# One wide matmul per weight block: a two-layer hybrid encoder whose column tiles stream both parts of the operand at once

## The chip, the cores and the metric

The kernel runs on one core of a Trainium2 chip. The metric is the device time of one execution in microseconds (us), of which the median over three runs is quoted. TensorE (PE) does the matmuls, VectorE (DVE) and ScalarE (ACT) the elementwise work, GpSimd (POOL) and SyncE (SP) mostly start transfers.

## The reference

Two identical layers and a final norm, on 256 tokens of 2048 channels. A layer normalises x, multiplies it by one wide input projection, feeds four token mixers (a short convolution A, attention B, a recurrence C in two directions, a convolution module D), projects each mixer's output, merges the four by sigmoid gates, and adds the output projection to x:

```python
h = rms_norm(x, norm_g)
proj = h @ w_in                      # 2048 x 15104, all mixers and gates
...
bp = jnp.einsum('bskc,kcd->bskd', ys, w_branch)
g = jax.nn.sigmoid(gates.reshape(b, s, N_BRANCH, D_MODEL) + b_gate)
merged = jnp.sum(g * bp, axis=2)
return x + merged @ w_out
```

All of it is float32 with a float32 accuracy.

## The kernel before

Everything is held channel-major: a tile is 128 channels by 256 tokens (`S` is 256). Weights come as a stream of chunks, each 128 x 1024 (512 KB): eight 128 x 128 blocks. A chunk is loaded into `raw`, ACT rounds it to `hi` (a float32r copy), and DVE makes `lo = raw - hi`; three `hi` and two `lo` buffers exist. The operand x is split in the same way into two float32r parts that lie side by side in a `slab`: `[128 channels, 4 tiles, hi | lo, 256 tokens]`.

A column tile (`tile_b`) is 128 output channels: two chunks, 16 blocks. For each block `passes` issues hi·x_hi and hi·x_lo, and after the eight blocks of a chunk lo·x_hi for each: 24 matmuls of 256 columns per chunk, all added up in one 256-column half of a PSUM bank. PSUM has eight banks: two under the tag `mg`, two under `mb`, four (`sd`) for the side computations. `tile_pair` puts two column tiles into the halves of one bank (gates and output projection), `tile_branch` does the same with one chunk for a mixer's projection (`mb`). Consumers read the PSUM tile directly.

The order of a layer's stream: three L tiles (low-rank inputs), the c_k, c_r, c_v tiles, k, v, the tiles of B and A, d_gate and d_val, then the merges M(0) and M(1) in turn, d_z, M(3) (mixer D's), c_z, M(2) (the recurrence's), and eight O pairs (output projection). The first tiles of a layer (`raw`) are computed from x before the norm and scaled by its reciprocal `rbc` afterwards.

Mixers are generators ("side computations"): after each main matmul `pump` lets one go on when a planner's clocks say that its inputs should be there, and when VectorE and ScalarE have little work ahead (`lead`). `drain` makes a merge wait in the planner until its mixer is finished. The planner's clock counts a matmul as columns / 2400 + 0.003 us. A scheduler then fixes the order on each engine; every engine runs its list strictly in order. `lo`/`hi` conversions carry high priority. All operations are recorded through one helper, so almost every row of the profile names its line, L199; the tile names tell the groups apart: `mg<-slab,hi` is a column tile's matmul with the weights' high part, `sd<-...` a side computation's, `arena<-mg` a read of a column tile out of PSUM.

Of the kernel before, what the change touches and what calls it, by code (L numbers as in the profile page):

```python
# [13 lines left out]
ALU = mybir.AluOpType  # L14
# [16 lines left out]
# columns of the per-channel parameter table  # L31
# [9 lines left out]
# columns of the constant table  # L41
# [14 lines left out]
def tile_order():  # L56
    """Column tiles of w_in that give channel-major outputs, in stream order."""
# [32 lines left out]
def stream_order():  # L90
    """The whole weight stream of a layer, in the order in which it is used."""
# [11 lines left out]
class Arena:  # L103
    """Addresses inside one SBUF tile, handed out and taken back in program order."""
# [12 lines left out]
    def get(self, words, keep=False, take=True):  # L117
        """keep: long-lived, from the bottom; others from the free run that fits best, if not just given back."""
# [4 lines left out]
        while i < self.n:  # L123
# [6 lines left out]
            if e - i >= m:  # L130
                # long-lived from the bottom, others from the top of the run that fits best
# [33 lines left out]
class Engine:  # L165
    """An engine of nc that keeps the clocks by which side computations are interleaved."""
# [43 lines left out]
class Kern:  # L210
# [39 lines left out]
    def a(self, shape, keep=False):  # L250
        words = int(np.prod(shape[1:]))
        if self.cur is None:
            # the main stream waits for side computations to give memory back
            t = self.now
            while not self.arena.get(words, keep, False) and self.now < t + 50:
                self.now += 0.2
                self.pump()
# [11 lines left out]
    def room(self, words):  # L269
        """Waits until the side computation that asks can have so much until it asks again."""  # L270
# [13 lines left out]
    def slab(self, shape, dt=F32):  # L284
        """8 KB per partition: operand tiles, and what the recurrence keeps until then."""
# [19 lines left out]
    # TensorE runs in program order. A side computation is a generator that yields before a step whose first  # L305
    # instructions use what the last step made; it goes on when that should be there: `now` is TensorE's clock,
    # `clk` when each engine has done what it was given, `due` when the step's results are there.
    def add(self, gen, lead=None):
        """lead: how much work VectorE and ScalarE may have before them when it goes on."""
        e = Side(gen, self.now, lead or self.LEAD)  # L310
        if self.cur:
            # a part of the computation that adds it, and so is its memory
# [5 lines left out]
    def rush(self):  # L318
        """What the recurrence waits for goes before other side computations."""
# [1122 lines left out]
```

## Time and profile before

| what | value |
|---|---|
| median of 3 runs | 2015.02 us (2013.86 to 2015.18) |
| profiled execution: span from its first to its last instruction | 2012.3 us |
| PE / PE weight loads | 1989.7 us (99%) / 1947.2 us (97%), 17122 of each |
| DVE | 1334.6 us (66%), 2143 instructions |
| ACT | 1176.3 us (58%), 2013 instructions |
| granted TensorE clock | 0.998, in all slices 9 of 10 or more: the 2.4 GHz level |
| traffic from HBM | 332.48 MB, 169 GB/s over the span |

How to read it: matmuls are pipelined, so the record of one is longer than the distance to the next. What a matmul costs in a stream is the distance between starts, which the timeline gives: a merged row has the start of its first record and the number of records, and the next row's start ends it.

### The profile page before, as it was taken

To read this page: it belongs to the slowest core of one execution; us is meant where nothing else is said; L and a number is where in the kernel's file an instruction comes from. 1 tells how busy PE (TensorE), PEld (TensorE's weight loads), DVE (VectorE), ACT (ScalarE), POOL (GpSimd) and SP (SyncE) were. 2 spreads that over 40 slices of the span, in tenths; PEclk is the share of its full clock that TensorE was granted. 3 is DMA by queue.
4 is the path that set the end of the run, shared out by engine and by line. 5 is a ranking of instruction groups with operands and counts; after the bars stand their busy time and mean duration, and the time that the engine had idled before them with its cause. 6 is when DMAs were issued, how large, how long until landed. Compare 5 with 4: busy or idle time off the path is not lost.

```text
span 2012.3 us, 41703 instructions
## 1 busy us (share of the span) xinstructions
PE 1989.7 (99%) x17122; PEld 1947.2 (97%) x17122; DVE 1334.6 (66%) x2143; ACT 1176.3 (58%) x2013; POOL 70.8 (4%) x115
## 2 busy tenths in 40 slices
PE   8999999999999999999999999999999999999997
PEld 7999999999999999999999999999999999999997
DVE  7666869866685445555676768797667845455554
ACT  6676665666546655444556766565764566544444
POOL 1001010000101000000000011000001100000000
PEclk9999999999999999999999999999999999999999
DMA  7555443445555445556655555444555634455553
GB/s 247 180 175 170 158 160 133 147 160 179 179 180 154 142 142 195 191 196 203 206 189 175 171 166 167 140 145 139 174 173 188 189 127 145 154 197 195 195 183 126
DMA packets 97727, 343.78 MB, mean 171 GB/s; under 512 B 11808, under 2 KB 12192, under 8 KB 97536
## 3 DMA queue, kind: packets, MB, share of 16 engines
q1 hardware_dynamic: 93312, 331.48, 49.3%
q0 software_dynamic: 3648, 8.59, 1.8%
q8 instruction: 134, 2.20, 0.4%
q10 hardware_dynamic: 576, 1.05, 0.1%
q14 instruction: 57, 0.47, 0.1%
HBM read 332.48 MB, written 8.39 MB: 169 GB/s over the span
## 4 chain that ended last, share of the span: by engine, by line
PE 98%; DVE 0%; ACT 0%; DMA 0%; issue 0%; DVEq 0%; SPq 0%; ACTq 0%
PE mg L199 78%; PE sd L199 10%; PE mb L199 10%; DMA arena<-xT 0%; DVE arena L199 0%; ACT slab L199 0%; DVE slab L199 0%; DVEq L1437 0%; ACT arena L199 0%; DVE lo L199 0%; ACT L178 0%; ACT hi L199 0%; SPq L199 0%; DVEq L199 0%; ACTq L199 0%
## 5 line engine op out<-in xcount | busy, mean ns | idle before, releaser
L199 PE MATMUL mg<-slab,hi 128*128 128x256 f32 x8704 | 1182.4, 285 | 9.7 <-ACT slab L199 8.6
L199 PEld LDWEIGHTS mg<-slab,hi 128*128 128x128 f32 x8704 | 1098.8, 192 | 20.9 <-ACT slab L199 8.6
L199 DVE TENSOR_TENSOR lo<-raw,hi 128x1024 fp32r<-128x1024 f32 x612 | 748.8, 1224 | 550.4 <-PE mg L199 372.3
L199 ACT ACTIVATE hi<-raw 128x1024 fp32r<-128x1024 f32 x612 | 646.9, 1058 | 647.5 <-PE mg L199 495.7
L199 PE MATMUL mg<-slab,lo 128*128 128x256 f32 x4352 | 636.0, 285 | 0.0
L199 PEld LDWEIGHTS mg<-slab,lo 128*128 128x128 f32 x4352 | 568.8, 192 | 5.6 <-issue 3.4
L199 DVE TENSOR_TENSOR arena<-arena 128x512 f32<-128x512 f32 (+18 forms) x365 | 156.1, 433 | 17.2 <-ACT arena L199 6.6
L199 DVE SCALAR_TENSOR_TENSOR arena<-arena,par 128x256 f32<-128x256 f32 x346 | 152.6, 478 | 6.4 <-ACT arena L199 4.9
L199 PE MATMUL mb<-slab,hi 128*128 128x256 f32 x1088 | 154.8, 284 | 0.0
L199 PEld LDWEIGHTS mb<-slab,hi 128*128 128x128 f32 x1088 | 141.0, 191 | 0.4
L199 PE MATMUL mb<-slab,lo 128*128 128x256 f32 x544 | 90.8, 286 | 0.0
L178 ACT ACT_TABLE_LOAD x62 | 79.5, 1283 | 16.6 <-PE sd L199 15.1
L199 ACT ACTIVATE arena<-arena 128x256 f32<-128x256 f32 (+4 forms) x155 | 77.5, 521 | 12.9 <-DVE arena L199 10.9
L199 PEld LDWEIGHTS mb<-slab,lo 128*128 128x128 f32 x544 | 75.8, 192 | 0.8
L199 ACT ACTIVATE arena<-sd 128x64 f32<-128x64 f32 (+4 forms) x146 | 44.1, 305 | 30.6 <-PE sd L199 28.0
L199 ACT ACTIVATE bdE<-sd 64x128 f32<-64x128 f32 (+1 forms) x192 | 52.1, 304 | 16.3 <-PE sd L199 15.1
L199 ACT ACTIVATE arena<-mg,b_gate 128x256 f32<-128x256 f32 x128 | 53.8, 467 | 5.2 <-DVE arena L199 3.2
L199 ACT ACTIVATE arena<-arena,par 128x256 f32<-128x256 f32 x88 | 42.4, 509 | 6.2 <-DVE arena L199 5.3
L199 DVE SCALAR_TENSOR_TENSOR arena<-arena,mb 128x512 f32<-128x512 f32 x64 | 43.5, 680 | 0.2
L199 PE MATMUL sd<-arena 96*128 96x256 f32 (+3 forms) x256 | 42.9, 322 | 0.0
L199 PE MATMUL sd<-arena,bdE 128*128 128x128 f32 (+1 forms) x288 | 42.7, 255 | 0.0
L199 ACT ACTIVATE arena<-sd,arena 128x128 f32<-128x128 f32 (+1 forms) x80 | 32.2, 405 | 17.1 <-PE sd L199 9.3
(95 smaller groups left out, 981.0 us busy)
## 6 DMA issues: line engine op xcount, KB each, us to landing
raw<-w SPq DMA_DIRECT2D x612, 512.0 KB, 3.3
arena<-xT SPq DMA_DIRECT2D x4, 512.0 KB, 8.0
scratch<-slab POOLq DMA_DIRECT2D x16, 128.0 KB, 3.1
scratch<-arena POOLq DMA_DIRECT2D x8, 256.0 KB, 3.6
arena<-xT SPq DMA_DIRECT2D x8, 256.0 KB, 4.1
x<-arena SPq DMA_DIRECT2D x8, 256.0 KB, 4.2
arena<-x SPq DMA_DIRECT2D x8, 256.0 KB, 3.6
arena<-lorab POOLq DMA_DIRECT2D x16, 96.0 KB, 3.3
```

Source lines behind the costliest of these rows:

```text
L178: return f(out)
L199: return f(out, *args, **kw)
```

## The change

`wide` replaces `passes` in `tile_b`: the hi part of a block multiplies both parts of x in one matmul of 512 columns, whose two halves land in the two halves of a whole PSUM bank; the lo pass still has 256 columns and adds to half 0. So a column tile takes a bank of its own and leaves two partial sums that must be added: `whole` copies half 1 to SBUF on ACT, then adds half 0 to it on DVE. `tile_pair` is gone; `mg` has three banks, `mb` one. Consumers read the sum from SBUF. The lines that lost only a comment or docstring are left out.

```diff
+    def wide(self, o, w, xs, first, last):
+        nc = self.nc
+        hi, lo = w
+        for i, (c, x) in enumerate(xs):
+            nc.tensor.matmul(o, hi[:, c * P:(c + 1) * P], x, start=first and i == 0, stop=False)
+            self.pump()
+        for i, (c, x) in enumerate(xs):
+            nc.tensor.matmul(o[:, 0], lo[:, c * P:(c + 1) * P], x[:, 0, :], start=False, stop=last and i == len(xs) - 1)
+            self.pump()
+
-    def tile_b(self, src, o=None):
-        if o is None:
-            # the first tiles wait for the reciprocal norms
-            self.tiles += 1
-            o = self.psum(*(("mb", 2) if self.tiles in (3, 4) else ("mg", 2)))[:, :S]
+    def tile_b(self, src):
+        self.tiles += 1
+        o = self.psum(*(("mb", 1) if self.tiles == 4 else ("mg", 3))).rearrange("p (a t) -> p a t", a=2)
         for j in range(2):
             w = self.chunk()
-            self.passes(o, w, [(k % 8, src[k // 4][:, k % 4]) for k in range(j * 8, j * 8 + 8)], j == 0, j == 1)
+            self.wide(o, w, [(k % 8, src[k // 4][:, k % 4]) for k in range(j * 8, j * 8 + 8)], j == 0, j == 1)
         return o
 
-    def tile_pair(self, src):
-        ps = self.psum("mg", 2)
-        for j in range(2):
-            self.tile_b(src, ps[:, j * S:(j + 1) * S])
-        return ps.rearrange("p (j t) -> p j t", j=2)
-
     def tile_branch(self, y):
-        ps = self.psum("mb", 2)
+        ps = self.psum("mb", 1)
...
+    def whole(self, out, ps):
+        nc = self.nc
+        nc.scalar.activation(out, ps[:, 1], AF.Copy)
+        nc.vector.tensor_tensor(out, ps[:, 0], out, ALU.add)
+        return out
...
     def evac(self, out, ps):
+        self.whole(out, ps)
         if self.raw:
-            self.nc.vector.tensor_tensor(out, ps, self.rbc, ALU.mult)
-        else:
-            self.nc.scalar.activation(out, ps, AF.Copy)
+            self.nc.vector.tensor_tensor(out, out, self.rbc, ALU.mult)
 
     def silu2(self, z):
-        s = self.a([P, S], True)
-        nc.scalar.activation(s, z, AF.Tanh, scale=0.5)
-        nc.vector.scalar_tensor_tensor(s, s, 1.0, z, ALU.add, ALU.mult)
+        s, y = self.a([P, S], True), self.a1()
+        self.whole(y, z)
+        nc.scalar.activation(s, y, AF.Tanh, scale=0.5)
+        nc.vector.scalar_tensor_tensor(s, s, 1.0, y, ALU.add, ALU.mult)
+        self.f(y)
...
-            nc.vector.tensor_tensor(u[:, 1:S + 1], got["a_cg"], ps, ALU.mult)
+            x = self.whole(self.a1(), ps)
+            nc.vector.tensor_tensor(u[:, 1:S + 1], got["a_cg"], x, ALU.mult)
+            self.f(x)
...
-            nc.scalar.activation(got[name], ps, AF.Tanh, scale=0.5)
+            self.whole(got[name], ps)
+            nc.scalar.activation(got[name], got[name], AF.Tanh, scale=0.5)
...
-            nc.vector.scalar_tensor_tensor(u[:, 15:S + 15], got["d_gate"], 1.0, ps, ALU.add, ALU.mult)
-            self.f(got.pop("d_gate"))
+            x = self.whole(self.a1(), ps)
+            nc.vector.scalar_tensor_tensor(u[:, 15:S + 15], got["d_gate"], 1.0, x, ALU.add, ALU.mult)
+            self.f(x, got.pop("d_gate"))
...
     def merge(self, l, br, g, acc, mT, gens):
-        ps = self.tile_pair(self.xT)
         z = self.a([P, 2, S], True)
         for j in range(2):
             o = br * KT + 2 * g + j
-            nc.scalar.activation(z[:, j], ps[:, j], AF.Tanh, scale=0.5, bias=self.bgh[:, o:o + 1])
+            self.whole(z[:, j], self.tile_b(self.xT))
+            nc.scalar.activation(z[:, j], z[:, j], AF.Tanh, scale=0.5, bias=self.bgh[:, o:o + 1])
...
     def project(self, l, mT):
             if g < 7:
-                ps = self.tile_pair(mT)
-                nc.vector.tensor_tensor(xr, ps, xr, ALU.add)
+                for j in range(2):
+                    ps = self.tile_b(mT)
+                    for i in range(2):
+                        nc.vector.tensor_tensor(xr[:, j], ps[:, i], xr[:, j], ALU.add)
...
                 for j in range(2):
                     ps = self.tile_b(mT)
-                    nc.vector.tensor_tensor(xr[:, j], ps, xr[:, j], ALU.add)
+                    for i in range(2):
+                        nc.vector.tensor_tensor(xr[:, j], ps[:, i], xr[:, j], ALU.add)
```

The planner and the scheduler work with the new sizes, so the order on the engines moves too. On PE in layer 0, where the first projection of mixer D (M(3), `mb_7844`, operand `slab_7130`) stands before the change:

```order
L199 MATMUL mg_7566<-slab_204,hi_7634 128x256 x3
L199 MATMUL mg_7566<-slab_203,lo_7635 128x256 x2
L199 MATMUL sd_7740<-consts,bdS_93 128x128
L199 MATMUL mg_7566<-slab_203,lo_7635 128x256 x2
L199 MATMUL mg_7566<-slab_204,lo_7635 128x256 x4
L199 MATMUL mb_7844<-slab_7130,hi_7732 128x256 x8
L199 MATMUL mb_7844<-slab_7130,lo_7733 128x256 x2
```

The same place on PE with the change (the projection is `mb_6485`, its operand `slab_5979`; `mg_6682` and `mg_6836` are column tiles of the merge steps that follow it):

```order
L199 MATMUL sd_6474<-bdX_79,slab_4524 32x32 x8
L199 MATMUL mb_6485<-slab_5979,hi_6373 128x256
L199 MATMUL mg_6682<-slab_203,lo_6629 128x256 x4
L199 MATMUL mg_6682<-slab_204,lo_6629 128x256 x4
L199 MATMUL mb_6485<-slab_5979,hi_6373 128x256
L199 MATMUL mg_6836<-slab_201,hi_6728 128x512 x4
L199 MATMUL mg_6836<-slab_202,hi_6728 128x512 x4
L199 MATMUL mb_6485<-slab_5979,hi_6373 128x256
L199 MATMUL sd_6504<-bdT_77,arena 32x32 x8
L199 MATMUL mb_6485<-slab_5979,hi_6373 128x256
L199 MATMUL sd_6517<-bdE_83,bdT_77 128x128 x2
L199 MATMUL sd_6529<-bdX_79,slab_4524 32x32 x8
```

Before, the projection's eight matmuls stood together behind the column tiles of their own merge step; now they are interleaved one by one with the tiles of the next two merge steps. On DVE, the four writes of that operand before the change:

```order
L199 SCALAR_TENSOR_TENSOR slab_7130<-arena,slab_7130 128x256
L199 SCALAR_TENSOR_TENSOR arena<-arena,mg_7356 128x256
L199 SCALAR_TENSOR_TENSOR arena<-arena 128x256 x2
L199 TENSOR_TENSOR lo_7463<-raw_7427,hi_7462 128x1024
...
L199 TENSOR_TENSOR lo_7570<-raw_7530,hi_7569 128x1024
L199 SCALAR_TENSOR_TENSOR slab_7130<-arena,slab_7130 128x256
L199 TENSOR_TENSOR lo_7635<-raw_7567,hi_7634 128x1024
```

And with the change, from its first write to its last on DVE:

```order
L199 SCALAR_TENSOR_TENSOR slab_5979<-arena,slab_5979 128x256
L199 TENSOR_TENSOR arena<-mg_6576,arena 128x256
L199 SCALAR_TENSOR_TENSOR arena<-arena 128x256
L199 TENSOR_TENSOR lo_6686<-raw_6626,hi_6685 128x1024
L199 SCALAR_TENSOR_TENSOR slab_5979<-arena,slab_5979 128x256
L199 TENSOR_TENSOR arena<-mg_6682,arena 128x256
L199 SCALAR_TENSOR_TENSOR arena<-arena 128x256 x3
L199 SCALAR_TENSOR_TENSOR slab_5979<-arena,slab_5979 128x256
L199 SCALAR_TENSOR_TENSOR arena<-arena 128x256 x2
L199 TENSOR_TENSOR bdE_85<-sd_6543,consts 128x2x64 x2
L199 SCALAR_TENSOR_TENSOR slab_5979<-arena,slab_5979 128x256
```

Before, the four writes were spread between the conversions of six chunks; now they follow each other with a single conversion between them, and come later in the stream of weights.

## Rows read from the trace of the kernel before

**Rows 1.** The page's head and busy times: engine, busy us, share, instructions.

```profile
span 2012.3 us, 41703 instructions
PE 1989.7 (99%) x17122; PEld 1947.2 (97%) x17122; DVE 1334.6 (66%) x2143; ACT 1176.3 (58%) x2013; POOL 70.8 (4%) x115
```

**Rows 2.** Waits of PE: who waited for whom: us in total, times, longest.

```profile
PE mg L199 <- ACT slab L199: 8.6, 1, 8.6
PE mg L199 <- DVE slab L199: 1.1, 3, 0.4
```

**Rows 3.** Groups by shape, PE: count, busy us, mean ns, idle before.

```profile
L199 PE MATMUL mg<-slab,hi 128*128 128x256 f32 x8704 | 1182.4, 285 | 9.7 <-ACT slab L199 8.6 <-DVE slab L199 1.1
L199 PE MATMUL mg<-slab,lo 128*128 128x256 f32 x4352 | 636.0, 285 | 0.0
...
L199 PE MATMUL sd<-part,rounded 128*128 128x512 f32 x48 | 18.2, 400 | 0.0
...
L199 PE MATMUL sd<-consts,bdS 128*128 128x128 f32 x48 | 13.0, 272 | 0.0
```

**Rows 4.** Timeline of PE in an O pair: start us, us, engine, operation, count.

```profile
960.38 1.12 PE L199 MATMUL mg<-slab,lo 128*128 128x256 f32 x8
961.34 2.08 PE L199 MATMUL mg<-slab,hi 128*128 128x256 f32 x16
963.26 0.40 PE L199 MATMUL mg<-slab,lo 128*128 128x256 f32 x2
```

**Rows 5.** Timeline of PE around three pairs of 512-column matmuls.

```profile
84.67 0.63 PE L199 MATMUL sd<-part,rounded 128*128 128x512 f32 x2
85.14 0.87 PE L199 MATMUL mg<-slab,hi 128*128 128x256 f32 x6
...
503.28 0.63 PE L199 MATMUL sd<-part,rounded 128*128 128x512 f32 x2
503.74 0.87 PE L199 MATMUL mg<-slab,hi 128*128 128x256 f32 x6
...
1496.42 0.63 PE L199 MATMUL sd<-part,rounded 128*128 128x512 f32 x2
1496.89 0.87 PE L199 MATMUL mg<-slab,hi 128*128 128x256 f32 x6
```

**Rows 6.** Groups by shape, DVE.

```profile
L199 DVE TENSOR_TENSOR lo<-raw,hi 128x1024 fp32r<-128x1024 f32 x612 | 748.8, 1224 | 550.4 <-PE mg L199 372.3 <-PE mb L199 70.8 <-issue 46.2
...
L199 DVE TENSOR_TENSOR arena<-mg,arena 128x512 f32<-128x512 f32 x14 | 9.6, 683 | 0.0
...
L199 DVE TENSOR_TENSOR arena<-mg,arena 128x256 f32<-128x256 f32 x18 | 7.4, 418 | 5.4 <-PE mg L199 4.6 <-ACT arena L199 0.8
```

**Rows 7.** Groups by shape, ACT.

```profile
L199 ACT ACTIVATE hi<-raw 128x1024 fp32r<-128x1024 f32 x612 | 646.9, 1058 | 647.5 <-PE mg L199 495.7 <-PE mb L199 65.8 <-issue 52.8
...
L199 ACT ACTIVATE arena<-mg 128x256 f32<-128x256 f32 x82 | 30.7, 375 | 3.6 <-PE mg L199 3.3
```

**Rows 8.** Stretches: us, busy us of PE, PEld, DVE, ACT, POOL; clock, DMA.

```profile
10.00:70.00 60.00, 59.74 (x478) 58.79 (x477) 50.73 (x84) 42.07 (x62) 2.97 (x5) 1.00 0.65 227
...
305.00:385.00 80.00, 80.00 (x736) 77.50 (x735) 72.63 (x150) 48.72 (x104) 0.00 (x0) 1.00 0.43 145
```

**Rows 9.** Timeline of DVE, the last write of mixer D's operand in layer 0.

```profile
626.27 1.23 DVE L199 TENSOR_TENSOR lo<-raw,hi 128x1024 fp32r<-128x1024 f32 x1 [1.42 <-PE mg L199]
627.41 0.42 DVE L199 SCALAR_TENSOR_TENSOR slab<-arena,slab 128x256 fp32r<-128x256 f32 x1
```

**Rows 10.** Timeline of PE at the first projection of M(3), layer 0.

```profile
640.08 1.12 PE L199 MATMUL mb<-slab,hi 128*128 128x256 f32 x8
...
641.37 0.59 PE L199 MATMUL sd<-bdT,arena 32*32 32x32 f32 x16
641.88 0.49 PE L199 MATMUL sd<-arena,bdE 128*128 128x128 f32 x2
```

**Rows 11.** Timeline of DVE after the last column tile.

```profile
1998.32 0.42 DVE L199 TENSOR_TENSOR arena<-mg,arena 128x256 f32<-128x256 f32 x1 [4.62 <-PE mg L199]
```

## The prediction

> **What bounds the kernel now.** I read the busy times first, then the waits of TensorE (PE), then its timeline, and DVE and ACT last. PE is busy for 1989.7 of 2012.3 us [rows 1] and waits 8.6 us for ACT once, for the first operand at the start, and 1.1 us for DVE in all [rows 2]. Nothing else is worth looking for on the other engines as long as PE is never kept waiting: the time is the sum of the distances between the starts of its matmuls. In a stretch of main matmuls sixteen starts of the hi pass take 963.26 - 961.34 = 1.92 us, and the eight of the lo pass before them 961.34 - 960.38 = 0.96 us: 0.120 us each, hi or lo [rows 4]. The records themselves last 285 ns [rows 3], which overlap and are no price. A chunk of 24 matmuls takes 2.88 us; of the 13,056 `mg` matmuls [rows 3] two thirds are hi.
>
> **What the wide matmul costs.** The change turns each pair of hi matmuls of a column tile into one of 512 columns. By the code a layer has 137 column tiles (3 L, 12 of C, k, v, 24 of A and B, 8 + 4 of D, 4 c_z, 64 gates, 16 O), 274 in both, each with 16 blocks: 4384 matmuls and as many weight loads go, and 4384 become wide. The trace has float32r matmuls of 512 columns, each with its own weight load: 48 from `part` [rows 3]. Where two stand together, the next row starts 0.47, 0.46 and 0.47 us after the first [rows 5]; a fourth pair, at 1077.82, repeats the first. That is 0.234 us each, by the mean of the four (1.87 / 8). Two of 256 columns cost 0.240. So the second matmul costs only some 6 ns more than its columns do, and this is all that a wide one saves: 0.240 - 0.2338 = 0.0062 us, times 4384 = 27.4 us. The rows resolve 0.01 us: by a pair of 0.47 the saving is 0.005 x 4384 = 21.9 us, by the pair of 0.46 it is 0.010 x 4384 = 43.8 us. I take the mean.
>
> The rows say that a weight load costs next to nothing: 512 columns with one load take nearly what 512 columns with two take. The Trainium skill ("TensorE: Matmul & The Clock Gate", section "Back-to-back issue gap") gives columns / 2.4 + 2.5 ns for an isolated matmul at full clock, 109 and 216 ns here. By that the saving would be 2.5 ns, 11 us in all; the trace has 120 and 234 ns instead, and the rows are what I use.
>
> **What is added.** `whole` reads the bank twice: an ACT copy of 128 x 256 out of PSUM is 0.375 us [rows 7], a DVE add with one operand in PSUM 0.418 us [rows 6]. By the order on the engines ACT gets 200 instructions more and DVE 288 more: 200 x 0.375 = 75 us, 288 x 0.418 = 120 us, less the O pairs' change from 14 adds of 0.683 us (9.6 us, rows 6), which are in the 288 as removed rows, so about 117 us. DVE goes from 1335 to some 1450 us, 73% of a span of 1990; ACT from 1176 to 1251 us, 63%. Neither becomes a bound on average. Where DVE is busiest, from 305 to 385 us, it has 7.4 us of 80 free; the 22 conversions there mean 11 tiles, 11 x 0.418 = 4.6 us, which still fits [rows 8]. The planner also counts the new operations and puts the side computations later. So I cost them at nothing on PE's path except in three places.
>
> The end: after the last matmul two adds stand where one of 0.42 us stood [rows 11]: + 0.4 us, certain.
>
> The start of a layer: its first eight tiles get a DVE add each, 3.3 us, in a stretch with 60 - 50.7 = 9.3 us free [rows 8]. I take 0; without that cover it is 3.3 us a layer, 6.7 us in all.
>
> The projection of mixer D, M(3): its last operand piece was written at 627.41 + 0.42 = 627.8 us and first needed at 640.08 [rows 9, 10], 12.3 us of slack. From d_gate to M(3) there are 44 tiles (8 of D, 32 gates, 4 d_z), so 44 x 0.418 = 18.4 us of new DVE work pushes the convolution back; if none of it fits into idle time, PE would be 6.1 us late. The order shows that it will be late: column tiles of the next two merge steps are moved ahead of the projection, whose matmuls follow one by one. Behind the first piece DVE has eleven instructions of 0.42 us and a conversion of 1.22 us before the last is there [rows 6, 9], 5.8 us without two small ones and ACT's part of each piece; PE has eight lo matmuls (0.96), eight wide ones (1.87) and four blocks of eight small ones (0.5 us for 16, rows 10: 1.0) to put between, 3.8 us. That leaves 2.0 us; the other bound is 6.1. PE runs in order, so all main matmuls queue behind that wait. I take 3.5, nearer to the count of instructions, with something for ACT's steps: 7.0 us in two layers, bounds 0 (if the first piece comes early) and 12.3.
>
> **Sum**, against the profiled execution's span of 2012.3 us: - 27.4 + 0.4 + 0 + 7.0 = - 20.0, so 1992.3 us. The median of the runs shown lies 2.7 us above that span, which is what surrounds it: 1995.0 us. At the ends: - 43.8 + 0.4 = - 43.4 gives 1971.6, and - 21.9 + 0.4 + 6.7 + 12.3 = - 2.5 gives 2012.5.
>
> **Rivals.**
>
> *Weight loads are the bound.* Loads are busy for 97% of the span [rows 1], and 4384 of 17122 (26%) go. If each 0.120 us were a load's slot and the stream only waited for it, a wide matmul would take only its stream, which is less than 0.234. The 512-column rows speak against it: the second of each pair loads while the first streams for twice as long, and yet nothing is gained [rows 5]. The nearest that rows allow is the pair of 0.46: 43.8 us less, with the 0.4 and half the wait 1971.6 + 3.5 + 2.7 = 1978 us. The Trainium skill ("Perfetto Trace Analysis", "Identifying the Most-Contended Engine") holds the busy share of weight loads to be the better measure of TensorE; with the first page's 216 ns for a wide one the saving would be 24 ns, 106 us, and the time about 1916. Chance 7%.
>
> *The gain is swallowed at the deadlines.* The lower saving, the full wait of 6.1 us at M(3) and the raw tiles uncovered: 2012.5 + 2.7 = 2015 us at the worst, 2009 with half of it. For it speaks that the order on PE was rearranged around M(3) at all; against it that PE now loses 1.1 us to DVE although DVE has stretches at 91% [rows 2, 8]. Chance 12%.
>
> *Slower: the recurrence's chain becomes the bound.* Its state goes step by step from PE to ACT and back, 48 steps in all (`bdS` on PE, rows 3), while the gate tiles run. ACT and DVE work strictly in order; if each step finds one new copy and one new add ahead of it, 0.375 + 0.418 = 0.79 us, and PE has nothing left to put between, 48 x 0.79 = 38 us come on top of 1995: 2033 us. It decides from the point where more than half the steps are hit (20 us). Against it: PE waits for no such step now, `rush` puts the chain first on both engines, and ACT is at 63%. Chance 8%.
>
> **How the numbers follow.** The forecast, wide matmuls at 0.234 us and a short wait at M(3), has 73%, and by itself a range of 1985 to 2005 us. This measurement can tell 0.2%, 4 us, from no change: faster is below 2011, slower above 2019. Faster: the forecast, the first rival and a third of the second, 73 + 7 + 4 = 84%. The same: the rest of the second, 8%. Slower: 8%. The range that leaves out 2 in 10 runs from 1981 to 2012.
>
> **What would show it.** Right: chunks of 8 x 0.234 + 0.96 = 2.83 us in the O stage; waits of PE for DVE or ACT at M(3) of a few us per layer and hardly anywhere else; DVE at 1450 us, ACT at 1250. Wrong: sixteen wide starts far from 3.74 us; or PE's rows of waits with many entries in the stretches of the recurrence; or `lo` conversions that PE waits for in the middle of a stage.

## The result, and the profile after

The changed kernel takes 2044.61 us (median of four runs, 2043.45 to 2047.59) against 2015.1 us for the kernel before on the same chip: 1.0151 times, interval 1.0137 to 1.0164. It is slower by 30 us, where 20 us less were forecast. The profiled execution spans 2043.6 us.

The head of the page after, its busy times, and the clock of TensorE in 40 slices; they answer to [rows 1]:

```profile
span 2043.6 us, 33386 instructions
PE 1973.2 (97%) x12738; PEld 1732.0 (85%) x12738; DVE 1421.7 (70%) x2431; ACT 1251.1 (61%) x2217; POOL 70.9 (3%) x115
PEclk9999998999999998999999999999999999989998
```

4384 matmuls and loads are gone, as announced; ACT is busy for 1251 us, as announced, and DVE for 1422, 28 us less than announced (its operations sum to 114 us more, as announced with 117, but the records of neighbours overlap). All of this fits, and the time does not. What is new stands in the list of PE's waits (who waited for whom, us in total, times, longest), which answers to [rows 2]:

```profile
PE mg L199 <- DVE arena L199: 29.1, 10, 6.0
PE mg L199 <- DVE slab L199: 9.5, 1, 9.5
PE sd L199 <- ACT part L199: 3.3, 2, 1.6
PE sd L199 <- ACT bdS L199: 2.6, 3, 1.5
...
PE mg L199 <- ACT hi L199: 2.3, 3, 1.8
PE mg L199 <- DVE lo L199: 2.1, 1, 2.1
```

Apart from the first operand (9.5 us, 8.6 before) PE waits for 48 us, where it waited for 1.6 (the 1.1 of [rows 2] and 0.5 for ACT, which those rows leave out). The first row is the new one: ten column tiles wait for `DVE arena`, that is, for the add that empties a bank.

The stream itself became faster than forecast. Timeline of PE in the output projection, which answers to [rows 4]:

```profile
949.91 3.82 PE L199 MATMUL mg<-slab,hi 128*128 128x512 f32 x16
953.57 2.08 PE L199 MATMUL mg<-slab,lo 128*128 128x256 f32 x16
955.48 2.68 PE L199 MATMUL mg<-slab,hi 128*128 128x512 f32 x11
```

Sixteen wide starts take 953.57 - 949.91 = 3.66 us, 0.229 each, and sixteen of the lo pass 1.91, 0.119 each. Over the whole trace the mean distance between two wide starts at full clock is 0.230. A wide matmul therefore saves some 0.010 us, not 0.0062.

Where the time went can be added up from the distances between the starts of matmuls, sorted by the kind of the first of the two (a wait counts with the matmul that stands before it):

| kernel | after a main matmul | after a side matmul (`sd`) |
|---|---|---|
| before | 1801.0 us | 189.8 us |
| after | 1781.7 us | 239.7 us |

The main stream gained 19.3 us, although some 4384 x 0.010 = 43.8 were to be had, and the side matmuls lost 49.9; with 0.9 us more at the start that is the 31.3 us between the spans.

One such wait shows how it comes about: the largest, at the end of the recurrence of layer 0. Rows are start, us, engine, operation, and in brackets idle time and who ended it. First PE:

```profile
807.94 1.52 PE L199 MATMUL sd<-part,rounded 128*128 128x512 f32 x2 [1.65 <-ACT part L199]
815.44 3.78 PE L199 MATMUL mg<-slab,hi 128*128 128x512 f32 x8 [5.98 <-DVE arena L199]
819.02 1.80 PE L199 MATMUL mg<-slab,lo 128*128 128x256 f32 x8
```

Then ACT in the same stretch:

```profile
809.49 1.28 ACT L178 ACT_TABLE_LOAD   x1 [1.60 <-PE sd L199]
810.78 0.69 ACT L199 ACTIVATE arena<-sd,eps 128x512 f32<-128x512 f32 x1
811.49 1.28 ACT L178 ACT_TABLE_LOAD   x1
812.78 0.63 ACT L199 ACTIVATE arena<-arena 128x512 f32<-128x512 f32 x1
814.17 0.38 ACT L199 ACTIVATE arena<-mg 128x256 f32<-128x256 f32 x1 [0.76 <-DVE arena L199]
```

And DVE:

```profile
813.45 0.69 DVE L199 TENSOR_TENSOR arena<-arena 128x512 f32<-128x512 f32 x1 [4.83 <-ACT arena L199]
814.17 0.88 DVE L199 SCALAR_TENSOR_TENSOR arena<-arena,par 128x256 f32<-128x256 f32 x2
814.97 0.42 DVE L199 TENSOR_TENSOR arena<-mg,arena 128x256 f32<-128x256 f32 x1
```

To be read from below: the next column tile needs a bank. The bank comes free with the add at 814.97, the add needs the copy of ACT at 814.17, and both stand in line, in order, behind the group norm of the recurrence, which holds ACT with two table loads and DVE with a wait of 4.83 us. No bank's contents are late by themselves; their readers are queued behind something that is.

The stall has a sequel: the eight wide matmuls behind it take 3.78 us in place of the usual 2.00. The view of two stretches (us, busy us of PE, PEld, DVE, ACT, POOL, then the granted clock, the busy share of DMA and GB/s) shows why:

```profile
815.50:819.00 3.50, 3.50 (x8) 2.75 (x9) 2.81 (x7) 1.56 (x4) 0.00 (x0) 0.50 0.17 60
830.00:840.00 10.00, 10.00 (x67) 9.13 (x66) 6.17 (x9) 4.87 (x7) 0.00 (x0) 1.00 0.61 197
```

Right after the idle time PE runs at the lower of its two levels, 1.2 GHz. The clock had fallen before this wait, at some 807 us, among side matmuls with waits of 0.8, 0.5 and 1.7 us between them: it is 0.73 from 806 to 808 us and 0.50 from 808 to 815. Ten such runs of 5 to 17 main matmuls (0.427 us a wide one, 0.213 a narrow one) follow the longer waits: 15.9 us above the usual distances. The kernel before has such a run at its start only.

### The profile page after: what moved, and what is told of

Read it like the earlier page. It is cut to its first block, busy times and chain, and to the rows that moved or that the text cites. A ratio compares the mean times of both kernels' runs of the same rounds, so it can differ in the third digit from the quotient of the medians.

```text
span 2043.6 us, 33386 instructions
## 1 busy us (share of the span) xinstructions
PE 1973.2 (97%) x12738; PEld 1732.0 (85%) x12738; DVE 1421.7 (70%) x2431; ACT 1251.1 (61%) x2217; POOL 70.9 (3%) x115
## 4 chain that ended last, share of the span: by engine, by line
PE 95%; ACT 2%; DVE 2%; issue 0%; DMA 0%; DVEq 0%; SPq 0%; ACTq 0%
PE mg L199 75%; PE sd L199 10%; PE mb L199 9%; DVE arena L199 1%; ACT arena L199 1%; DVE lo L199 1%; ACT L178 0%; ACT hi L199 0%; DMA arena<-xT 0%; ACT bdE L199 0%; ACT L199 0%; DVE slab L199 0%; DVEq L1457 0%; ACT bdS L199 0%; ACT part L199 0%
## 5 line engine op out<-in xcount | busy, mean ns | idle before, releaser
L199 PE MATMUL mg<-slab,hi 128*128 128x512 f32 x4368 | 1136.3, 400 | 41.0 <-DVE arena L199 29.1
L199 PEld LDWEIGHTS mg<-slab,hi 128*128 128x128 f32 x4368 | 796.0, 191 | 190.3 <-DVE arena L199 23.1
L199 PE MATMUL mg<-slab,lo 128*128 128x256 f32 x4368 | 622.1, 286 | 2.1 <-DVE lo L199 2.1
L199 PEld LDWEIGHTS mg<-slab,lo 128*128 128x128 f32 x4368 | 590.7, 192 | 37.8 <-DVE lo L199 2.2
L199 DVE TENSOR_TENSOR arena<-arena 128x512 f32<-128x512 f32 (+15 forms) x389 | 165.8, 432 | 38.8 <-ACT arena L199 29.4
L199 PE MATMUL mb<-slab,hi 128*128 128x256 f32 (+1 forms) x1040 | 157.7, 286 | 0.5 <-DVE slab L199 0.5
L199 DVE TENSOR_TENSOR arena<-mg,arena 128x256 f32<-128x256 f32 x305 | 126.8, 417 | 23.0 <-ACT arena L199 19.5
L199 ACT ACTIVATE arena<-mg 128x256 f32<-128x256 f32 x241 | 90.6, 377 | 48.6 <-PE mg L199 31.3
L199 ACT ACTIVATE arena<-arena 128x256 f32<-128x256 f32 (+4 forms) x195 | 93.7, 498 | 33.1 <-DVE arena L199 28.6
L199 ACT ACTIVATE arena<-arena,b_gate 128x256 f32<-128x256 f32 x128 | 64.2, 503 | 56.6 <-DVE arena L199 56.1
```

What stands on the lines that cost most here:

```text
L199: return f(out, *args, **kw)
```

## The experiments

The table gives all runs with a time, against the kernel before on the same chip (2014.5 to 2015.1 us); "readers" is the number of operations that empty a bank of a column tile. "Plan" is what the planner's clock was told, which decides after which tile a side step is issued; the scheduler still fixes the order on each engine afterwards, so that the same plan does not mean the same order there.

| kernel | matmul | readers | banks | plan | us | ratio (interval) |
|---|---|---|---|---|---|---|
| after | wide | 2 | 3+1 | own | 2044.6 | 1.0151 (1.0137-1.0164) |
| one reader | wide | 1 | 3+1 | own | 2007.6 | 0.9966 (0.9953-0.9979) |
| two readers, narrow | narrow | 2 | 2+2 | own | 2039.2 | 1.0119 (1.0102-1.0136) |
| emptied first | wide | 2 | 3+1 | own | 2047.2 | 1.0162 (1.0146-1.0177) |
| one tag of banks | wide | 2 | 4 | own | 2039.6 | 1.0122 (1.0107-1.0137) |
| plan of before 2.8% dearer | narrow | 1 | 2+2 | x 1.028 | 2030.4 | 1.0074 (1.0059-1.0089) |
| wide 2.8% cheaper | wide | 2 | 3+1 | x 0.972 | 2017.7 | 1.0014 (1.0005-1.0024) |
| measured distances | wide | 2 | 3+1 | 0.12, 0.23 us | 2024.9 | 1.0050 (1.0033-1.0067) |
| one reader, old plan | wide | 1 | 3+1 | of before | 2008.9 | 0.9967 (0.9956-0.9978) |
| after, old plan | wide | 2 | 3+1 | of before | 2033.8 | 1.0097 (1.0082-1.0112) |
| narrow, old plan | narrow | 2 | 2+2 | of before | 2026.6 | 1.0060 (1.0045-1.0075) |
| one reader, old plan, one tag | wide | 1 | 4 | of before | 2009.6 | 0.9976 (0.9966-0.9986) |
| after, old plan, one tag | wide | 2 | 4 | of before | 2008.8 | 0.9968 (0.9957-0.9980) |
| banks alone | narrow | 1 | 3+1 | of before | 2013.9 | 0.9994 (0.9984-1.0003) |
| no lo conversion | wide | 2 | 3+1 | own | 2007.2 | 0.9961 (0.9946-0.9976) |
| every fourth without | wide | 2 | 3+1 | own | 2032.9 | 1.0095 (1.0078-1.0111) |
| wide late only | 1024 wide | 2 | 2+2 | of before until M(2) | 2009.5 | 0.9973 (0.9963-0.9984) |
| wide late, banks in turn | 1024 wide | 2 | 2+2 | of before until M(2) | 2003.1 | 0.9944 (0.9927-0.9960) |
| the same and 20 early tiles | 1664 wide | 2 | 2+2 | of before | 2009.2 | 0.9972 (0.9961-0.9982) |

### First: is it the second reader, the banks, or the line they stand in?

One reader:

```diff
 def whole(self, out, ps):
-    nc.scalar.activation(out, ps[:, 1], AF.Copy)
-    nc.vector.tensor_tensor(out, ps[:, 0], out, ALU.add)
+    nc.scalar.activation(out, ps[:, 0], AF.Copy)
```

(and where a bank had been read in place, `ps[:, 0]` is read in place again)

> The kernel after with one reader for each bank: only the first half of the bank is read, in one operation as in the kernel before; the second half (the product of the high part of the weights with the low part of x) is computed and left out of the result. The wide matmuls, the two bank tags (3 and 1) and the planner's rules stay. Theory 1 (the second reader of each bank, queued in order behind other work on ACT and DVE, keeps PE waiting, and PE then runs at half clock for a while): the waits fall from 48 us to under 10, the half-clock matmuls go with them, and the time is about 2015 - 43 = 1972 us, at most 1985. Rival 2 (three banks of one tag and one of the other, in place of two and two, hold PE up): stays at 2035 to 2045. Rival 3 (the planner prices a wide matmul wrongly and puts side work too late): some 2030 to 2045. Rival 4 (a wide matmul itself is no gain, or brings the clock down): 2015 or more.

It took 2007.6 us. Without the second reader the time is 37 us less, but the planner counts fewer operations and the order moved as well: counted in narrow matmuls, a side matmul stands on average some 131 main matmuls earlier than in the kernel after. And 1972 was missed by as much: with one reader PE still waits 19 us besides the start. The sum of distances says where: after main matmuls 1758.7 us, 42 less than before, about the whole gain; after side matmuls 225.7, 36 us more than before. So the first theory is at best half of it. A piece of the chain, PE and then ACT:

```profile
239.15 3.78 PE L199 MATMUL sd<-kz,arena 128*128 128x512 f32 x4 [1.21 <-DVE arena L199]
243.79 3.77 PE L199 MATMUL mg<-slab,hi 128*128 128x512 f32 x8 [0.86 <-ACT arena L199]
```

```profile
242.44 0.47 ACT L199 ACTIVATE arena<-sd,arena 128x256 f32<-128x256 f32 x1 [6.13 <-DVE arena L199]
...
243.35 0.38 ACT L199 ACTIVATE arena<-mg 128x256 f32<-128x256 f32 x1
```

Here too a bank's reader (243.35) stands on ACT behind side work (the softmax, which waited 6.13 us), and PE runs side matmuls one after the other with nothing between them.

Two readers with narrow matmuls, the kernel before otherwise:

```diff
-    nc.scalar.activation(out, ps, AF.Copy)
+    nc.scalar.activation(out, ps, AF.Copy)
+    nc.vector.tensor_tensor(out, ps, out, ALU.max)
```

> The other half of the change alone: the kernel before with narrow matmuls and its own banks, where each column tile's bank (but for the 32 tiles that go into a silu, and the output projection) is read twice, by an ACT copy and then by a DVE maximum of the bank and the copy, so that values are as before. Theory 1: the second reader costs PE waits here too, some 30 to 60 us with the half clock behind them: 2040 to 2075 us. Rival 2 (banks) and rival 3 (price of wide matmuls), rival 4 (the wide matmul): nothing of theirs is in this kernel, so 2015 to 2020 us.

2039.2 us, just under the range of theory 1: the readers cost 24 us without any wide matmul. But the planner counts them, so the order changed as well; this is taken apart below.

Emptied first:

```diff
+    with self.tc.high_priority():
         nc.scalar.activation(out, ps[:, 1], AF.Copy)
         nc.vector.tensor_tensor(out, ps[:, 0], out, ALU.add)
```

> The kernel after, with the two operations that empty a bank put ahead of all ready work on ACT and DVE by the scheduler's priority. Theory 1, in the form that the two readers stand in line behind side work that could as well come later: most of the 29 us of waits of main matmuls for DVE go, and part of the half clock: 2000 to 2020 us. In the form that whatever is put ahead only moves the lateness to the side work (waits of `sd` and `lo` grow instead): 2035 to 2050. Rivals 2 and 3: 2035 to 2045.

2047.2 us, and 31.1 us of waits for DVE in place of 29.1. Priority alone does not bring the readers forward: over the 273 column tiles under the tag `mg` the add that empties the bank starts on average 4.5 us after the tile's last matmul, with and without it. Nor did the lateness go to the side work, whose waits are 14.3 us (14.4 in the kernel after). Why it has no effect stays open.

One tag of banks:

```diff
-    o = self.psum(*(("mb", 1) if self.tiles == 4 else ("mg", 3)))
+    o = self.psum("mg", 4)
```

(and the same for the branch projections)

> The kernel after, with all four banks under one tag, so that column tiles and the branches' projections take the next free one of four. Rival 2 (the division of banks into three and one is the cause): 1985 to 2010 us. Theory 1: a fourth bank gives at most one tile, 5.6 us, more room, but only where a branch's projection is not in it; some of the ten waits get shorter: 2025 to 2045. Rivals 3 and 4: 2040 to 2045.

2039.6 us, 5 us less: with this plan the division of the banks is not the cause.

### Second: the order

> The kernel before with the same work on every engine; only the number by which the planner advances its clock for a float32r matmul is 2.8% larger, so that its clock stands to the chip's as it does in the kernel after (a wide matmul is planned at 0.216 us and takes 0.230, a narrow one at 0.110 and 0.120). Theory 5, formed after the run with one reader per bank came to 2008 and not 1972: the order of the kernel before, with no waits at all, fits one cadence of the stream, and any other cadence moves side work on the three engines in line so that PE meets it late; then this kernel, without a single instruction added, loses 10 to 40 us: 2025 to 2055. Theory 1 in its first form (only the added readers cost): 2013 to 2018. Rival 3 (the planner's price): 2020 to 2035.

```diff
-    k.now += n * ... / 2400 + 0.003
+    k.now += (n * ... / 2400 + 0.003) * (1 if rhs.dtype == F32 else 1.028)
```

Not one instruction more, and 15.5 us slower. The longest rows of PE's waits besides the start (9.4 us), 11.0 us in all, where the kernel before had 1.6:

```profile
PE sd L199 <- ACT bdS L199: 3.5, 2, 1.8
PE mg L199 <- ACT arena L199: 3.5, 4, 1.1
PE sd L199 <- ACT arena L199: 1.9, 3, 0.7
```

So the nearly empty list of [rows 2] is no property of the work, but of one order that fits.

The kernel after, with the plan's price of a wide matmul 2.8% lower, and with measured distances:

```diff
+    ... * (0.972 if n == 512 and rhs.dtype != F32 else 1)
```

> The kernel after, with a wide matmul planned 2.8% cheaper, so that planned time stands to chip time as in the kernel before (0.914). Rival 3 (it is the planner's price of a wide matmul): waits fall by half or more, 2000 to 2020 us. Theory 5 in its general form (the order is not tuned for this stream, in whichever direction a number is moved): another set of stalls of the same size, 2030 to 2060. Theory 1: 2035 to 2050.

> The kernel after, with the planner's clock advanced by the measured distances (0.120 us for 256 columns, 0.230 for 512), so that planned and chip time of the stream agree; side steps then come after fewer matmuls. Rival 3 (wrong price of the matmul): 1995 to 2020 us. Theory 5: another order with stalls of its own, 2030 to 2070. Theory 1: 2035 to 2055, since the added readers are all still there.

2017.7 and 2024.9 us, 27 and 20 us less than after, by a number in the plan alone. The first was forecast by the rival (the price), the second by neither; one price is lower, the other higher than in the kernel after, and both help. It is not that the price was wrong in one direction: orders differ by up to 27 us, and the one of the kernel after is a poor one.

### Third: the same plan for all

A wide matmul is told to the planner as two narrow ones, and the second reader is not told at all, which was meant to put the side steps after the same tiles as before.

```diff
-    k.now += n * ... / 2400 + 0.003
+    k.now += n * ... / 2400 + (0.006 if k.wides else 0.003)
...
-    nc.vector.tensor_tensor(out, ps[:, 0], out, ALU.add)
+    self.tc.nc.vector.tensor_tensor(out, ps[:, 0], out, ALU.add)
```

> Wide matmuls, one reader for each bank (the second half of the bank, the product of the high part of the weights with the low part of x, is left out of the result), and the plan of the kernel before: a wide matmul advances the planner's clock by what two narrow ones did, so that side steps stand after the same tiles as before. Theory 5 (the loss of the run with one reader, 36 us short of 1972, is the order that the planner's changed clock gave): the waits go, 1970 to 1990 us. If the order does not matter: 2005 to 2010 as in that run. If the stream, now faster by 3% than the plan assumes, meets side work late all the same: 1990 to 2005.

> The kernel after in full, with both readers of each bank, and the plan of the kernel before: a wide matmul counts as two narrow ones, and of the two operations that empty a bank the planner counts only what the kernel before had there. Theory 5: most of the 30 us lost against the kernel before were the new order: 1980 to 2005 us. Theory 1 (the added readers themselves delay side work and banks, in any order): 2025 to 2050, and the difference to the run with one reader and the same plan is then the price of the readers.

> The kernel before with narrow matmuls, each bank read twice as in the first run of that kind (copy, then maximum of bank and copy; silu tiles and the output projection as before), but the second reader is not counted by the planner, so that the plan is that of the kernel before to the step. Theory 5: the 24 us of that run were its order; here 2015 to 2025 us. Theory 1: the readers cost the same, 2035 to 2050.

2008.9, 2033.8 and 2026.6 us. With the old plan and one reader, wide matmuls still bring 6 us and not some 44. This does not refute the theory of the order, because the order on PE did not become that of the kernel before. Counted by the main matmuls ahead of it (a wide one as two), a side matmul stands on average 103 later than before in the first of these kernels (four chunks), 78 later in the second, and 148 later in the kernel after; only in the narrow one is it nearly in place, 9 earlier. The last state step of the recurrence in layer 0 stands behind 218 chunks before, 229 in both wide kernels here, and 232 in the kernel after. With these plans the readers cost 12 us in a narrow stream and 25 in a wide one. The loss in the run with one reader stands mostly in one place of each layer, PE first, then DVE:

```profile
474.79 1.11 PE L199 MATMUL mg<-slab,lo 128*128 128x256 f32 x8
486.28 2.04 PE L199 MATMUL mb<-slab,hi 128*128 128x256 f32 x8 [10.39 <-DVE arena L199]
```

```profile
484.67 0.87 DVE L199 SCALAR_TENSOR_TENSOR arena<-arena,par 128x256 f32<-128x256 f32 x2
485.46 0.68 DVE L199 SCALAR_TENSOR_TENSOR arena<-arena,mb 128x512 f32<-128x512 f32 x1
```

The reader of the one bank for branch projections (`mb`, 485.46) comes after a block of side work on DVE; PE waits 10.4 us for that bank. So the banks were tried again.

> The run with wide matmuls, one reader for each bank (second half left out of the result) and the plan of the kernel before (2008.9 us), with four banks under one tag for column tiles and branch projections. If the single bank of the branch projections is the cause: both waits of 10.4 us and the half-clock matmuls behind them go, 1980 to 1990 us. If side work is late in any case: some other wait takes their place, 2000 to 2009.

> The kernel after in full with the plan of the kernel before (2033.8 us), with four banks under one tag. Its waits were 18.8 us of column tiles and 7.3 us of branch projections for DVE, and 13 us of side matmuls. If the banks are the cause: both DVE rows go, 2000 to 2012 us. If the readers are: only the 7.3 us and what follows them, 2022 to 2030.

> The kernel before in all but the division of its four banks: three for column tiles and one for branch projections, as in the kernel after, in place of two and two. Narrow matmuls, one reader, the same plan. If one bank for the branch projections is too few in itself: 5 to 20 us more, 2020 to 2035. If it is too few only for a faster stream: 2014 to 2017.

2009.6, 2008.8 and 2013.9 us. Alone, three banks and one cost nothing; with one reader, four under one tag only move the wait (12.3 us for a column tile now); with both readers they bring 25 us, and with them the readers cost nothing any more. In both wide kernels the side matmuls still stand over 100 main matmuls later than before. What the banks are worth depends on the order that they meet, like everything else here.

### Fourth: does DVE lack the time?

Four wide kernels with one or two readers end at 2007 to 2010 us, each with other waits. The view of the busiest stretch of the kernel after, which answers to the second of [rows 8]:

```profile
305.00:385.00 80.00, 77.06 (x594) 66.59 (x593) 74.56 (x163) 44.83 (x110) 0.00 (x0) 0.94 0.36 119
```

DVE is free for 5.4 us of 80, while PE stands still for 2.9 and runs at a clock of 0.94. The next two kernels take work from DVE and leave the readers, the banks and what the planner is told as in the kernel after.

```diff
-    nc.vector.tensor_tensor(lo, raw, hi.bitcast(F32), ALU.subtract)
+    lo = hi      # of every chunk; in the second kernel, of every fourth
```

> The kernel after, with the conversion of the weights' low part left out (612 operations of 1.22 us on VectorE, 747 us): the low pass multiplies the high part once more in its place, so that TensorE, ScalarE, the banks and the planner's clock are as they were. If VectorE's lack of time is the cause: its busy time falls to 675 us, the waits of 48 us and the half-clock matmuls go, 1975 to 1990 us. If the cause is the order itself, with chains of side steps and ScalarE behind them: 2015 to 2045.

> The same with every fourth chunk only: VectorE is busy for some 1235 us, 100 us less than in the kernel before. If VectorE's time is the cause and its amount in the dense stretches decides: about half of the loss goes, 2005 to 2025 us. If what counts is that an operation stands in line behind a conversion at all, little changes: 2030 to 2045.

2007.2 and 2032.9 us: 37 us less with DVE at 37% of the span, 12 less with a quarter of that relief. The second time lies in the range of the rival, by which the place in line counts and not the amount of work, and DVE's busy time says the same: with 1257 us it is 77 us below the kernel before, which is 18 us faster. The adds come earlier after a tile's last matmul, 3.0 and 3.9 us on average in place of 4.5. The order on PE did not stay quite fixed either: a side matmul stands on average 28 main matmuls (counted as above), some one chunk, away from its place in the kernel after in the first and 41 in the second, so that part of the gain can be the order's. Distances after main matmuls fall to 1757.1 us in the first, 43.9 less than before, about all of 4384 x 0.010; as some 7 us at half clock are still in them, the match to a tenth is chance. The waits that remain in the first of the two:

```profile
PE mg L199 <- DVE arena L199: 13.8, 4, 6.0
...
PE sd L199 <- ACT arena L199: 4.5, 7, 1.1
PE sd L199 <- ACT part L199: 3.3, 2, 1.6
```

All waits of layer 0 between 100 and 300 us are gone, and from 300 to 780 us 3.6 us are left. What stays, 8.3 us in each layer, is the end of the recurrence shown above (6.0 for the bank, 1.6 for `part`): there DVE itself waits for ACT, and its free time is of no use. The upper bound of the expectation, 1990, was missed by this and by some side matmuls that follow one another.

### A version that beats both

Wide matmuls only where no side work is left to be late:

```diff
-        ps = self.tile_pair(self.xT)
+        ps = None if br == 2 else self.tile_pair(self.xT)     # M(2): wide, as is O
```

> The kernel before, with wide matmuls only where no side computation is left to be late: the 32 column tiles of the merge steps M(2) and the 32 of the output projection, in both layers; the rest of the stream, its banks and its order until then are those of the kernel before. The first theory and theory 5 (below) alike: 64 x 16 wide matmuls save 0.010 us each, 10.2 us, and two adds in place of one at the end cost 0.4 us: 2005 us, 2003 to 2008. Rival 4 (a wide matmul saves only 0.006 us or brings the clock down): 6 us less at most, 2009 or more. If the second reader of a bank costs PE time even with ACT and DVE nearly idle: 2015 or more.

2009.5 us, 5.4 less in place of 10. Until M(2) its course is that of the kernel before, but for 0.9 us at the start. PE and DVE where it loses, at the first tiles of the output projection:

```profile
920.17 1.10 PE L199 MATMUL mg<-slab,lo 128*128 128x256 f32 x8
923.47 1.86 PE L199 MATMUL mg<-slab,hi 128*128 128x512 f32 x7 [2.19 <-DVE arena L199]
```

```profile
921.11 0.42 DVE L199 TENSOR_TENSOR arena<-mg,arena 128x256 f32<-128x256 f32 x1
921.44 1.22 DVE L199 TENSOR_TENSOR lo<-raw,hi 128x1024 fp32r<-128x1024 f32 x1
922.57 1.08 DVE L199 TENSOR_TENSOR arena<-mg,arena 128x256 f32<-128x256 f32 x3
```

A bank waits for its two adds, and these behind a conversion. With banks of both tags in turn:

```diff
-        ps = self.tile_w(mT)
+        ps = self.tile_w(mT, ("mg", "mb")[j])
```

> The kernel with wide matmuls in M(2) and the output projection alone, which came to 2009.5 us because the first tiles of the projection waited twice for a bank (2.2 us each, with half-clock matmuls behind it in the second layer). Here the projection's tiles take banks of both tags in turn, four in all. If it was the banks: both waits go and the time is 2004 us (2003 to 2006), the full saving of 1024 x 0.0094 = 9.6 us less 0.4 at the end. If the wait is for the operand of the projection (the longer way from the last gate tile to it): 2008 to 2010.

2003.1 us (2002.3 to 2004.5), 0.9944 (0.9927 to 0.9960): the fastest of all. Here the order did stay: but for 10 of 2434, every side matmul stands behind the same main matmuls as before. Distances after main matmuls sum to 1789.0 us, 12.0 less than before for 1024 wide matmuls; after side matmuls 190.4, as before. All of PE's waits:

```profile
PE mg L199 <- ACT slab L199: 9.3, 1, 9.3
PE sd L199 <- ACT arena L199: 1.0, 1, 1.0
PE mg L199 <- DVE arena L199: 0.6, 1, 0.6
```

Twenty more tiles of each layer, the ones after its first eight:

> The best version so far (wide in M(2) and the output projection, 2003 us) with the 20 column tiles of each layer that follow the first eight made wide too, where the run with the plan of the kernel before was still gaining; the planner counts them as two narrow ones. 40 x 16 x 0.0098 = 6.3 us less: 1997 us if the rest of the order stays; 2003 to 2015 if the added readers shift side work behind them into PE's way.

2009.2 us: 6 us more in place of 6 less. At the end of d_z, at some 620 us, this kernel is 4.0 us behind the kernel before, where it had been 1 to 2 ahead at 137 us; the rest of the order did not stay.

## Why the prediction was wrong

**The step that failed** is "So I cost them at nothing on PE's path except in three places", the price of the added copies and adds. They cost the most of all: PE waits 48 us in some thirty places, 29.1 of them in ten waits for the add that empties a bank, 15.9 us more go at half clock behind the waits (by the sums of distances, which hold both, 49.9 us are lost after side matmuls). One reader in place of two takes 37 us off. What stood behind the price was a subtraction of free time, "which still fits", and it asked the wrong question. In the stretch from 305 to 385 us 7.4 us were free and 4.6 us of adds came in [rows 8]; the same edit also takes 22 x 8 x 0.010 = 1.8 us from the stretch, for its 22 chunks have eight wide matmuls each, so 1.0 us of 78 is left. But PE stands still for only 2.9 of its 48 us there, and with every fourth conversion left out DVE works less than before and the time is still 18 us longer. So free time alone did not decide. In the stalls shown it was the moment at which the reader of a bank or a step of a chain came up in its line. How much of the 30 us is due to the readers themselves and how much to the order that the planner and the scheduler made of them is not shown, because no wide kernel changed the one and held the other fixed; in the narrow kernel with the old plan, whose order is nearly that of before, the readers cost 12 us.

**The saving of a wide matmul** was mis-sized the other way: 27.4 us forecast, about 44 by the rows of the kernel after (0.229 to 0.230 us against 0.240). The right value was the upper bound, the pair of 0.46 us [rows 5]; four records with steps of 0.01 us do not carry a mean to a thousandth. This is also the price of the rival by which weight loads are the bound. Whether its mechanism holds is not settled: 0.230 for 512 columns fits a stream of 0.115 for each 256 behind a load's slot of 0.120, and as well a stream with a fixed 0.010 for each matmul. The Trainium skill ("TensorE: Matmul & The Clock Gate", section "Back-to-back issue gap") gives 216 ns for an isolated matmul of 512 columns at full clock; the stream here has 229 to 230. The Trainium skill names the busy share of weight loads as one of two measures of how near TensorE is to its limit ("Perfetto Trace Analysis", section "Identifying the Most-Contended Engine"); here it fell from 97% to 85% with a quarter of the loads gone, while the time rose by 1.5%, so by itself it did not tell the way.

**The wait at M(3)** was forecast as 3.5 us a layer for the late operand of the projection. PE's waits there in layer 0 (640 to 672 us):

```profile
PE mg L199 <- ACT hi L199: 1.8, 1, 1.8
PE sd L199 <- ACT bdT L199: 1.0, 1, 1.0
PE mb L199 <- DVE slab L199: 0.5, 1, 0.5
```

Only the last row is that operand: 0.5 us once, and none in layer 1. The other two are a column tile's weights and a step of the recurrence. That the three add up to 3.3 us is luck. The wait had been singled out because its operand had a time that could be read; banks had none.

**The end** was right: from the add after the last column tile to the end of the span it was 2012.3 - 1998.3 = 14.0 us [rows 1, 11], and is 14.4 from the first of the two adds now (2043.6 - 2029.2). **The start of a layer** cost nothing, as taken.

**The rivals.** Of the slower one (a chain of side steps with a new copy and add ahead of each) the direction is right and the time near (2033 us against 2045), but by luck: PE does not wait 48 times for the state, which costs it 2.6 us in three waits, but some thirty times, ten of them for a bank. "The gain is swallowed at the deadlines" gave 2009 us, the time of several kernels here, but by a smaller saving and a wait at M(3), and they have neither. Two of the rivals' sums add the 2.7 us around the span twice: 1971.6 + 3.5 is 1975 us and not 1978, and the worst case of the second is 2012.5 and not 2015; no chance hangs on it. What I had not seen is the clock: 15.9 us at half clock behind the waits.

**Not seen at all** was the bank. The change hands a bank to two engines one after the other, so that it comes free only when both lines have moved (814.17 on ACT, 814.97 on DVE in the stall shown). The prediction asked whether the engines have time, and not what stands ahead in their lines when a bank is due.

**What stays open.** The parts do not add up: depending on the other two, the second readers cost between nothing and 37 us, the banks between nothing and 25, and the plan between nothing and 27. The loss of the kernel after can be taken away in two ways (DVE relieved: 37 us; the plan of before with four banks under one tag: 36 us, with DVE as busy as ever), so no single one of them is shown to be the cause. In all wide kernels but the two with late wide matmuls alone the order on PE moved with the edit; the full change in the order of the kernel before was not run. Why so different kernels all stop at 2007 to 2010 us, with 225 to 226 us after side matmuls in four of them, is not settled; a common bound was not shown. An order made for the wide stream was tried only by two prices of a matmul, which brought 20 and 27 us; setting the planner's other constants anew was not tried.

## What to carry to other kernels

Where an engine works in order and the order was laid down for one cadence, free time on an engine is no proof of cover: a faster main stream shortens it, and what counts is when an operation comes up in its line. For every buffer that the change gives a second reader, ask what stands ahead of that reader in line when the buffer is due. And where a change helps one operation everywhere, try it first where nothing else runs: 1024 of the 4384 wide matmuls brought 12 us, all of them cost 30.

## What was not expected of the hardware

- Float32r matmuls of 512 columns stand 0.229 to 0.230 us apart in a long stream with a weight load each, those of 256 columns 0.119 to 0.120.
- After its longer idle times PE's main matmuls ran at the lower clock level for 5 to 17 of them, 1.0 to 2.5 us each time: in the kernel after 15.9 us on top of 48 us of waits.
- A change of 2.8% in a number that only orders the work costs 15.5 us, 0.7%, in a kernel whose engines all do the same work as before.
